# A two-layer conformer trunk: three opening products by rows, and attention corners without a padded key tile

## The chip, the core and the metric

The kernel runs on one core of one Trainium2 chip. A core has TensorE (PE, matrix products into PSUM), VectorE (DVE), ScalarE (ACT), GpSimd (POOL) and SyncE (SP, which here only issues DMA transfers). Each engine works through its own queue in order and waits for others by semaphores. The metric is the device time of one execution in microseconds. Three runs of the kernel before took 2230.79, 2237.22 and 2239.99 us; the median is 2237.22.

## The reference

The input is 512 frames of 1024 numbers; 16 learned meta tokens stand in front, so the stream `h` has 528 tokens. There are two layers, all in fp32:

```
h += 1/2 * (silu(n(h) @ w_gate) * (n(h) @ w_up)) @ w_down        # first feed-forward, width 2816
u = n(h);  q, k, v, a, b, g_sb, g_conv = split(u @ w_in)
A = stick_breaking_attention(q, k, v) @ w_attn_out               # 8 heads of 64
B = conv_module(a, b) @ w_conv_out                               # causal, 31 taps
h += (sigmoid(g_sb) * A + sigmoid(g_conv) * B) @ w_out
h += 1/2 * (silu(n(h) @ w_gate2) * (n(h) @ w_up2)) @ w_down2     # second feed-forward
out = n(h)[16:]                                                  # n is an RMS norm with gains
```

Stick-breaking attention: the weight of key s for query t is sigmoid(z_ts) times the product of (1 - sigmoid(z_tj)) over all j between s and t, strictly causal. So each block of scores goes through a softplus, and sums of it over later keys are taken off before the exponential.

## The kernel before

The stream lies with channels on partitions: `h[k]`, eight tiles of 128 channels by 528 tokens. Every fp32 product is three products of split operands: a number is cast to a shorter type (`wh`, `uh`: high part, ScalarE) and the rest is kept (`wl`, `ul`: low part, VectorE); hi x hi, hi x lo and lo x hi are added in PSUM. `split` (line 69) does this for a weight of 128 x 1024, `prepare` (line 279) for a tile of the stream with its gain; `prepare` also takes the square (`squares`, line 293), and the squares are added up in `nsum`, by GpSimd but for the last two of eight. A product with ones and a short chain on VectorE and ScalarE makes `rstd` of the sum. The norm's factor is applied to the products' results, so products start before it is known.

The feed-forward (`ffn`, line 413) goes over 22 blocks of 128 columns of `w_gate` and `w_up`. The first two (`PLAIN`) are plain: 48 products for a matrix and a block, 24 weight tiles by two token halves. The other blocks go in pairs through `quad` (line 470): seven groups of 24 products in place of eight, which need sums of weight tiles and sums of token halves (`sums`, line 329: per pair of stream tiles two activations, four short VectorE products and two splits). After blocks 4, 10, 16 and 22 follow the down products (`down`, line 526). In the first feed-forward all eight `prepare` stand first, then the four `sums` ahead of the plain blocks, which the scheduler puts in between.

The attention (`attend`, line 689) works on a pair of heads. Keys and queries are split into high and low parts, scores go in four pieces of 128 keys. The last 16 keys and the first 16 tokens are a corner of their own: GpSimd copies 64 x 16 pieces of `kf` into a zeroed tile `kz`, one plain fp32 product per column group gives the scores of both heads (lines 711 to 719), and a bf16 product of `identb` and `masksb` adds the mask. There are four head pairs in each of two layers, so eight corners.

A scheduler orders the instructions of each engine by priority and readiness; `priority(EARLY)` and `priority(LATE)` move a piece. Weights are fetched by SP into three buffers `wr` in the order of the list `units`, three units ahead of use. In PSUM, `ps` has two buffers and `pb` and `pe` have one each.

Of the kernel before, what the change touches and what calls it, by code (L numbers as in the profile page):

```python
# [7 lines left out]
F32 = mybir.dt.float32  # L8
# [16 lines left out]
PLAIN = 2  # L25
ORDER = (0, 4, 1, 5, 2, 6, 3, 7)
CONV = 512
# [3 lines left out]
EARLY = 3000  # L31
CONV_STEP = 4
# [21 lines left out]
def kernel(ctx, tc, hT, par, const, wg1, wu1, wd1, win, wao, wco, wout, wg2, wu2, wd2, out):  # L54
# [68 lines left out]
    for l in range(DEPTH):  # L123
        for fi, (wg, wu, wd) in enumerate(((wg1, wu1, wd1), (wg2, wu2, wd2))):
# [12 lines left out]
            for m in range(PLAIN):  # L137
                units += [((f"g{fi}", l, m), wg[l, m], 8), ((f"u{fi}", l, m), wu[l, m], 8)]
            m = PLAIN
# [7 lines left out]
    state = {"prep": 0, "use": 0, "fetch": 0, "out": 0, "sums": 0, "raw": 1}  # L147
# [3 lines left out]
    def pieces(n, block=None):  # L151

        key, src, nk = units[n]
        if nk in QUAD:
            wg, wu, m = src
            k, c = RAW_OF[block or nk]
            return [(4 * e, 4 * e + 4, w[m + c, :, 4 * k:4 * k + 4]) for e, w in enumerate((wg, wu))]
        return [(a, b, src[:, a:b]) for a, b in (((0, 2), (2, nk)) if n == 0 else ((0, nk),))]
# [9 lines left out]
    def fetch():  # L168
        while state["fetch"] < len(fetches) and state["out"] < state["raw"]:
# [25 lines left out]
    def prep_unit():  # L195
# [7 lines left out]
        if nk not in QUAD:  # L203
            raw = raws.pop(key)
            for a, b in ((0, 2), (2, nk)) if n == 0 else ((0, nk),):
                split(raw[:, a:b], hi[:, a:b], lo[:, a:b])
# [12 lines left out]
        if state["raw"] > 1:  # L219
            fetch()  # L220
# [20 lines left out]

    prm = cst.tile([P, N_PAR], F32, name="prm")
    nc.sync.dma_start(prm, par)
    h = [hpool.tile([P, T], F32, name=f"h{k}") for k in range(KD)]
    for n, k in enumerate(ORDER):
        nc.sync.dma_start(h[k], hT[:, k])
        if n in (0, 3):
            prep_unit()
    state["raw"] = RAW
# [10 lines left out]
    dve.tensor_copy(trir, cc[:, C_TRI:C_TRI + P])  # L260
    identb = cst.tile([P, P], BF16, name="identb")
    dve.tensor_copy(identb, ident)
    maskb = cst.tile([P, 240], BF16, name="maskb")
    dve.tensor_copy(maskb, cc[:, C_MASK:C_MASK + 240])
    masksb = cst.tile([64, 32], BF16, name="masksb")
    dve.tensor_copy(masksb, cc[:64, C_MS:C_MS + 32])
# [12 lines left out]
    def prepare(tp, k, ncol, st, mode=FULL, alloc=None):  # L279
# [10 lines left out]
        if alloc is not None and 0 <= k - 4 < 3:  # L290
            sums(alloc, k - 4, st, mode)

    def squares(tp, k, st, mode):
# [6 lines left out]
        else:  # L300
# [3 lines left out]
            eng = dve if n >= KD - 2 else pool  # L304
            eng.tensor_tensor(out=tri(st["sum"], mode), in0=tri(a, mode), in1=tri(sq, mode), op=ALU.add)
# [23 lines left out]
    def sums(alloc, kk, st, mode):  # L329
# [12 lines left out]
        parts = []  # L342
        for r in (r1, r2):
            hi, lo = (two(stile(kk, n), mode) for n in ("sh", "sl"))
            split(r, hi, lo)
            parts.append((hi, lo))
        st.setdefault("S", {})[kk] = parts
# [65 lines left out]
    def ffn(l, fi, st, mode, after):  # L413
# [3 lines left out]
        with tc.tile_pool(name=f"ffn{l}{fi}", bufs=1, reuse_waits="tile") as fp, \  # L417
# [8 lines left out]
            if first:  # L426
                for k in ORDER:
                    prepare(fp, k, 0, st)
# [27 lines left out]
            def gate_up(m):  # L456
                pg = plain("pe" if m else "ps", "g", m)[:, :, :TH]
                if m == 0:
                    norm["r"] = rms_rstd(fp, st, ptile("pb"), mode)
                pu = plain("pb" if m else "ps", "u", m)[:, :, :TH]  # L460
# [5 lines left out]
                parts(u, m)  # L466

# [94 lines left out]
            with tc.tile_pool(name=f"quad{l}{fi}", bufs=1, reuse_waits="tile") as sp:  # L562
                quads.update(pool=sp, of=(fi, l))
                fetch_sums()
                for m in range(PLAIN):
                    if m == 0:
                        for kk in range(0 if first else 3, 4):
                            sums(gtile, kk, st, mode)
                    gate_up(m)
                m = PLAIN  # L570
# [13 lines left out]
    def mixer(l, st, omode, after):  # L584
        last = omode == XO
        with ExitStack() as es:
# [53 lines left out]
            with tc.tile_pool(name=f"psm{l}", bufs=3, space=bass.MemoryType.PSUM, reuse_waits="tile") as psp, \  # L640
# [29 lines left out]
                with tc.tile_pool(name=f"att{l}", bufs=1, reuse_waits="tile") as ap_:  # L670
# [18 lines left out]
                    def attend(i, qf, kf, vf):  # L689
# [21 lines left out]
                        kz = ap_.tile([P, 2, P], F32, tag="kz", bufs=1, name="kz")  # L711
                        pool.memset(kz, 0.0)
                        zs = ztile()[:, 0, :]
                        for c, t0 in ((0, SEQ), (1, 0))[:ncor]:
                            for hh in range(2):
                                r = slice(64 * hh, 64 * hh + 64)
                                pool.tensor_copy(kz[r, c, 32 * hh:32 * hh + 16], kf[r, t0:t0 + 16])  # L717
                            pe.matmul(zs[:, c * 16:c * 16 + 16], kz[:, c, :], qf[:, t0:t0 + 16],
                                      start=(c == 0), stop=False, skip_group_check=True)
# [231 lines left out]
```

## Time and profile before

| | |
|---|---|
| median of three runs | 2237.22 us |
| the profiled execution | 2235.04 us |
| its span, first to last instruction | 2233.3 us |
| PE, DVE, ACT, POOL busy | 2190.7, 1618.3, 1037.6, 467.7 us |
| TensorE's mean granted clock | 0.994 |

All rows below are from the profiled execution, with times from the start of its span. A matmul's duration overlaps its neighbour's; the distance of starts tells the rate. A granted clock of 1 is 2.4 GHz, 0.5 is 1.2 GHz.

### The profile page before, as it was taken

The page shows a single profiled execution, that of the slowest core. Times are in us where ns is not written, and L with a number is a line of the kernel's source. Part 1 is how long each engine was busy: PE and PEld are TensorE (multiplying, and loading weights), DVE is VectorE, ACT ScalarE, POOL GpSimd, SP SyncE. Part 2 cuts the span into 40 slices and gives each one's busy share as a digit, 9 for nine tenths or more (in the row PEclk, how much of TensorE's full clock was granted, in tenths as well). Part 3 has the DMA queues.
Part 4 walks back from the last instruction along what each step waited for, and adds up shares of the span by engine and source line. Part 5 has one row for each costly group of instructions (what it writes and reads, how often), then busy time and mean ns, then how long its engine had stood idle before and what let it go on. Part 6 is the DMA issues. An engine that isn't in the chain of part 4 may idle for free.

```text
span 2233.3 us, 39375 instructions
## 1 busy us (share of the span) xinstructions
PE 2190.7 (98%) x16140; PEld 2065.1 (92%) x16140; DVE 1618.3 (72%) x2113; ACT 1037.6 (46%) x1448; POOL 467.7 (21%) x394
## 2 busy tenths in 40 slices
PE   7999999999999999999999999999999999999997
PEld 6999999988899999999999999999777788999896
DVE  8767686877777768576887676868777777776684
ACT  6344345355535444353554443552665365444353
POOL 3322321100000132313123223211000002322222
PEclk9999999999999999999999999999999999999999
DMA  7565533211122275474265654332111225575532
GB/s 220 151 164 136 145 102 116 86 38 48 55 75 89 92 180 150 131 181 128 86 162 150 170 144 131 107 112 86 48 48 57 89 92 145 150 179 140 151 107 74
DMA packets 120261, 263.26 MB, mean 118 GB/s; under 512 B 13200, under 2 KB 15504, under 8 KB 120080
## 3 DMA queue, kind: packets, MB, share of 16 engines
q1 hardware_dynamic: 96240, 217.99, 29.9%
q0 software_dynamic: 23040, 41.95, 11.7%
q8 instruction: 127, 2.08, 0.4%
q10 hardware_dynamic: 800, 0.79, 0.1%
q14 instruction: 54, 0.44, 0.1%
HBM read 258.58 MB, written 2.10 MB: 117 GB/s over the span
## 4 chain that ended last, share of the span: by engine, by line
PE 93%; DVE 3%; POOL 1%; issue 1%; ACT 1%; DMA 0%; DVEq 0%; SPq 0%; POOLq 0%; ACTq 0%
PE ps L604 24%; PE ps L484 15%; PE pb L484 15%; PE ps L238 10%; PE pb L238 6%; PE pe L238 6%; PE pe L484 5%; PE z L604 2%; PE po L787 2%; PE ps L449 2%; PE z L777 1%; PE pe L449 1%; PE pb L449 1%; POOL kz L717 1%; PE z L760 1%
## 5 line engine op out<-in xcount | busy, mean ns | idle before, releaser
L71 ACT CAST wh<-wr 128x1024 fp32r<-128x1024 f32 (+3 forms) x369 | 352.1, 954 | 600.4 <-PE ps L604 178.5
L72 DVE TENSOR_TENSOR wl<-wr,wh 128x1024 fp32r<-128x1024 f32 (+3 forms) x369 | 439.4, 1191 | 73.0 <-ACT wh L71 67.3
L71 ACT CAST wh<-s 128x1024 fp32r<-128x1024 f32 x160 | 167.9, 1050 | 280.0 <-DVE s L214 84.6
L72 DVE TENSOR_TENSOR wl<-s,wh 128x1024 fp32r<-128x1024 f32 x160 | 218.5, 1365 | 58.8 <-ACT wh L71 58.0
L544 POOL TENSOR_TENSOR h<-h,dt 128x528 f32<-128x528 f32 (+1 forms) x96 | 179.6, 1875 | 252.3 <-DVE dt L542 252.3
L604 PE MATMUL ps<-uh,wh 128*128 128x264 f32 (+1 forms) x864 | 223.0, 315 | 0.4 <-DVE kf L677 0.3
L604 PE MATMUL ps<-ul,wh 128*128 128x264 f32 (+1 forms) x864 | 218.8, 310 | 0.0
L604 PE MATMUL ps<-uh,wl 128*128 128x264 f32 (+1 forms) x864 | 215.4, 309 | 0.0
L192 POOL DMA_DIRECT2D s<-wg x80 | 74.6, 933 | 542.6 <-DMA s<-wg 265.9
L632 DVE SCALAR_TENSOR_TENSOR y<-uc,prm,y 128x528 f32<-128x528 f32 (+1 forms) x240 | 183.4, 764 | 4.7
L484 PE MATMUL pb<-sh,wh 128*128 128x264 f32 (+1 forms) x640 | 181.8, 284 | 2.7 <-ACT pb L503 2.7
L484 PE MATMUL ps<-uh,wh 128*128 128x264 f32 (+1 forms) x640 | 181.3, 283 | 1.0 <-DVE g L463 1.0
L484 PE MATMUL pb<-sh,wl 128*128 128x264 f32 (+1 forms) x640 | 182.2, 285 | 0.0
L484 PE MATMUL pb<-sl,wh 128*128 128x264 f32 (+1 forms) x640 | 182.0, 284 | 0.0
L484 PE MATMUL ps<-uh,wl 128*128 128x264 f32 (+1 forms) x640 | 181.3, 283 | 0.0
L484 PE MATMUL ps<-ul,wh 128*128 128x264 f32 (+1 forms) x640 | 181.3, 283 | 0.0
L604 PEld LDWEIGHTS ps<-uh,wh 128*128 128x128 f32 x864 | 145.3, 191 | 20.9 <-issue 10.5
L604 PEld LDWEIGHTS ps<-ul,wh 128*128 128x128 f32 x864 | 145.5, 192 | 13.0 <-issue 6.8
L604 PEld LDWEIGHTS ps<-uh,wl 128*128 128x128 f32 x864 | 143.6, 191 | 12.1 <-issue 5.9
L238 PE MATMUL ps<-al,wh 128*128 128x264 f32 (+1 forms) x616 | 142.7, 301 | 0.5 <-DVE al L72 0.2
L238 PE MATMUL ps<-ah,wh 128*128 128x264 f32 (+1 forms) x616 | 141.8, 300 | 0.0
L238 PE MATMUL ps<-ah,wl 128*128 128x264 f32 (+1 forms) x616 | 141.7, 300 | 0.0
(276 smaller groups left out, 6042.9 us busy)
## 6 DMA issues: line engine op xcount, KB each, us to landing
wr<-wd SPq DMA_DIRECT2D x96, 384.0 KB, 3.6
wr<-win SPq DMA_DIRECT2D x72, 512.0 KB, 3.3
wr<-wg SPq DMA_DIRECT2D x120, 256.0 KB, 3.0
wr<-wu SPq DMA_DIRECT2D x120, 256.0 KB, 3.5
s<-wg SPq DMA_DIRECT2D x80, 256.0 KB, 4.5
s<-wu SPq DMA_DIRECT2D x80, 256.0 KB, 5.3
s<-wg POOLq DMA_DIRECT2D x80, 256.0 KB, 5.2
s<-wu POOLq DMA_DIRECT2D x80, 256.0 KB, 6.8
```

The costliest lines, as they stand in the source:

```text
L71: act.copy(hi, x)
L72: dve.tensor_tensor(out=lo, in0=x, in1=f(hi), op=ALU.subtract)
L192: pool.dma_start(t[:, a:b], src, accum_op=ALU.add)
L238: pe.matmul(ps[:, c, :n], wt[:, k0 + k, :], xt[:, s:s + n], start=(k == 0 and pi == 0), stop=(k == nk - 1 and pi == 2))
L449: pe.matmul(ps[:, e, :TH], wt[:, k, :], xt[:, s], start=(k == ORDER[0] and pi == 0), stop=(k == ORDER[-1] and pi == 2))
L484: pe.matmul(ps[:, e, :TH], wt[:, 4 * e + kk, :], xt, start=start and kk == 0 and pi == 0, stop=kk == 3 and pi == 2, skip_group_check=True)
L544: pool.tensor_tensor(out=tri(h[j], mode), in0=tri(h[j], mode), in1=tri(t, mode), op=ALU.add)
L604: pe.matmul(ps, wt[:, k0 + k, :], xt[:, s], start=(n == 0 and pi == 0), stop=(n == nk - 1 and pi == 2))
L632: t = dve.scalar_tensor_tensor(out=y, in0=uc[i][:, c0 + k:k + T], scalar=col(w0 + k), in1=y, op0=ALU.mult, op1=ALU.add)
L717: pool.tensor_copy(kz[r, c, 32 * hh:32 * hh + 16], kf[r, t0:t0 + 16])
L760: pe.matmul(z[:, hh, :n], KH[hh][:, ks], qq, start=True, stop=False, skip_group_check=True)
L787: pe.matmul(po[c, q0 - META:q0 - META + n], v[:, t, c], a[:, hh, :], start=False, stop=(t == 0), skip_group_check=True)
```

## The change

In the first feed-forward the first three matrices (gate and up of block 0, gate of block 1) are computed together, row tile by row tile, as the stream arrives. Stream tiles and weight pieces are fetched in five steps (`BEGIN`), in that order. Four blocks are plain there, and the `sums` come with blocks 2 and 3. All square sums go to VectorE, in every feed-forward and mixer. In the other feed-forwards `head` takes the place of `gate_up`, with `pb` and `pe` exchanged, and the sums of the next block have a later priority (`SOON`). The corner products read `kf` and `qf` directly, one product for a head and column group, and the mask product opens the buffer.

```diff
-PLAIN = 2
+PLAIN, PLAIN_FIRST = 2, 4
+BEGIN = ((0, 1), (1, 2), (2, 4), (4, 6), (6, 8))
+SOON = 150
...
     prm = cst.tile([P, N_PAR], F32, name="prm")
-    nc.sync.dma_start(prm, par)
+    nc.scalar.dma_start(prm[:, :N_NORM], par[:, :N_NORM])
     h = [hpool.tile([P, T], F32, name=f"h{k}") for k in range(KD)]
-    for n, k in enumerate(ORDER):
-        nc.sync.dma_start(h[k], hT[:, k])
-        if n in (0, 3):
-            prep_unit()
-    state["raw"] = RAW
+    begin = [wpool.tile([P, 8, P], F32, tag="wr", bufs=RAW, name="wr") for _ in range(3)]
+    for a, b in BEGIN:
+        for k in range(a, b):
+            nc.sync.dma_start(h[k], hT[:, k])
+        for raw, (_, src, _) in zip(begin, units):
+            nc.sync.dma_start(raw[:, a:b], src[:, a:b])
+    state.update(prep=3, use=3, fetch=3)
+    nc.sync.dma_start(prm[:, N_NORM:], par[:, N_NORM:])
...
         if alloc is not None and 0 <= k - 4 < 3:
-            sums(alloc, k - 4, st, mode)
+            with priority(SOON):
+                sums(alloc, k - 4, st, mode)
...
-            eng = dve if n >= KD - 2 else pool
-            eng.tensor_tensor(out=tri(st["sum"], mode), in0=tri(a, mode), in1=tri(sq, mode), op=ALU.add)
+            dve.tensor_tensor(out=tri(st["sum"], mode), in0=tri(a, mode), in1=tri(sq, mode), op=ALU.add)
...
-            def gate_up(m):
-                pg = plain("pe" if m else "ps", "g", m)[:, :, :TH]
-                if m == 0:
-                    norm["r"] = rms_rstd(fp, st, ptile("pb"), mode)
-                pu = plain("pb" if m else "ps", "u", m)[:, :, :TH]
+            def evac(m, pg, pu):
                 g = gtile()
...
+            def head():
+
+                pg = plain("ps", "g", 0)
+                norm["r"] = rms_rstd(fp, st, ptile("pe"), mode)
+                sums(gtile, 3, st, mode)
+                evac(0, pg[:, :, :TH], plain("ps", "u", 0)[:, :, :TH])
+                pg = plain("pb", "g", 1)
+                evac(1, pg[:, :, :TH], plain("pe", "u", 1)[:, :, :TH])
+
+            def first_head():
+
+                ws = [tuple(wpool.tile([P, 8, P], F32R, tag=n, bufs=4, name=n) for n in ("wh", "wl")) for _ in begin]
+                pss = [ptile(t) for t in ("ps", "ps", "pb")]
+                for a, b in BEGIN:
+                    for k in range(a, b):
+                        prepare(fp, k, 0, st)
+                    for raw, (hi, lo) in zip(begin, ws):
+                        split(raw[:, a:b], hi[:, a:b], lo[:, a:b])
+                    for k in range(a, b):
+                        xh, xl = st["u"][k]
+                        for ps, (hi, lo) in zip(pss, ws):
+                            for pi, (wt, xt) in enumerate(((hi, xh), (hi, xl), (lo, xh))):
+                                for e, s in enumerate(toks):
+                                    pe.matmul(ps[:, e, :TH], wt[:, k, :], xt[:, s], start=(k == 0 and pi == 0),
+                                              stop=(k == KD - 1 and pi == 2))
+                norm["r"] = rms_rstd(fp, st, ptile("pe"), mode)
+                g = fp.tile([P, T], F32, tag="up", bufs=3, name="up")
+                act.copy(th(g), pss[2][:, :, :TH])
+                evac(0, pss[0][:, :, :TH], pss[1][:, :, :TH])
+                evac(1, th(g), plain("pb", "u", 1)[:, :, :TH])
+                for m, tags in ((2, ("ps", "ps")), (3, ("pe", "ps"))):
+                    pg, pu = (plain(t, n, m)[:, :, :TH] for t, n in zip(tags, "gu"))
+                    evac(m, pg, pu)
+                    for kk in range(2 * m - 4, 2 * m - 2):
+                        sums(gtile, kk, st, mode)
...
-                        kz = ap_.tile([P, 2, P], F32, tag="kz", bufs=1, name="kz")
-                        pool.memset(kz, 0.0)
                         zs = ztile()[:, 0, :]
+                        pe.matmul(zs[:, :w], identb[:64, :], masksb[:, :w], start=True, stop=False, skip_group_check=True)
                         for c, t0 in ((0, SEQ), (1, 0))[:ncor]:
                             for hh in range(2):
                                 r = slice(64 * hh, 64 * hh + 64)
-                                pool.tensor_copy(kz[r, c, 32 * hh:32 * hh + 16], kf[r, t0:t0 + 16])
-                            pe.matmul(zs[:, c * 16:c * 16 + 16], kz[:, c, :], qf[:, t0:t0 + 16],
-                                      start=(c == 0), stop=False, skip_group_check=True)
-                        pe.matmul(zs[:64, :w], identb[:64, :64], masksb[:, :w], start=False, stop=False,
-                                  skip_group_check=True)
+                                pe.matmul(zs[32 * hh:32 * hh + 16, c * 16:c * 16 + 16], kf[r, t0:t0 + 16],
+                                          qf[r, t0:t0 + 16], start=False, stop=False, skip_group_check=True)
```

TensorE's queue at the very start, before and then now; `ps_270` is the gate of block 0 before, and now `ps_156`, `ps_157` and `pb_158` are the three matrices (`x2`: both token halves).

```order
L449 MATMUL ps_270<-uh0_133,wh_87 128x264 x2
L449 MATMUL ps_270<-ul0_134,wh_87 128x264 x2
L449 MATMUL ps_270<-uh0_133,wl_88 128x264 x2
L449 MATMUL ps_270<-uh4_139,wh_87 128x264 x2
L449 MATMUL ps_270<-ul4_140,wh_87 128x264 x2
L449 MATMUL ps_270<-uh4_139,wl_88 128x264 x2
```

```order
L489 MATMUL ps_156<-uh0_159,wh_150 128x264 x2
L489 MATMUL ps_156<-ul0_160,wh_150 128x264 x2
L489 MATMUL ps_156<-uh0_159,wl_151 128x264 x2
L489 MATMUL ps_157<-uh0_159,wh_152 128x264 x2
L489 MATMUL ps_157<-ul0_160,wh_152 128x264 x2
L489 MATMUL ps_157<-uh0_159,wl_153 128x264 x2
L489 MATMUL pb_158<-uh0_159,wh_154 128x264 x2
L489 MATMUL pb_158<-ul0_160,wh_154 128x264 x2
L489 MATMUL pb_158<-uh0_159,wl_155 128x264 x2
L489 MATMUL ps_156<-uh1_189,wh_150 128x264 x2
```

One tile of the stream now serves 18 products before the next is needed; before it served 6.

VectorE's queue after the three matrices, now: `wl_422` is the low part of `u` of block 1, `wl_428` and `wl_434` those of block 2, `wl_440` that of the gate of block 3; `nt` and `rstd` are the norm, `g_404` the first evacuation, which frees `ps_156`.

```order
L74 TENSOR_TENSOR wl_422<-wr_415,wh_421 128x1024
L74 TENSOR_TENSOR wl_428<-wr_417,wh_427 128x1024
L365 TENSOR_SCALAR nt_393<-pe_389 128x528
L74 TENSOR_TENSOR wl_434<-wr_419,wh_433 128x1024
L366 TENSOR_TENSOR nt_394<-rstd_390 128x528
L367 SCALAR_TENSOR_TENSOR nt_394<-nt_394,nt_393 128x528
L368 SCALAR_TENSOR_TENSOR rstd_390<-nt_394,rstd_390 128x528
L74 TENSOR_TENSOR wl_440<-wr_425,wh_439 128x1024
L461 TENSOR_TENSOR g_404<-ps_156,rstd_390 128x528
```

Before, the products of the token halves stood among the steps of the norm; now three weight splits do:

```order
L341 SCALAR_TENSOR_TENSOR g_238<-h6_81,prm_73,g_237 128x264
L361 TENSOR_TENSOR nt_345<-rstd_341 128x528
L72 TENSOR_TENSOR sl_246<-g_237,sh_245 128x528
L362 SCALAR_TENSOR_TENSOR nt_345<-nt_345,nt_344 128x528
L72 TENSOR_TENSOR sl_250<-g_238,sh_249 128x528
L341 SCALAR_TENSOR_TENSOR g_254<-h3_78,prm_73,g_253 128x264
```

The `g` and `sl` rows here belong to the sums of token halves, which now come with blocks 2 and 3.

TensorE's queue at the first corner of the first layer, before and then now; `z_5208` and `z_5229` are the corner's buffers, `ps_5132`, `ps_5133`, `ps_5155` and `ps_5156` the projection of `v` around it.

```order
L604 MATMUL ps_5133<-ul0_4140,wh_4931 128x264
L604 MATMUL ps_5133<-uh0_4139,wl_4932 128x264
L604 MATMUL ps_5133<-uh4_4146,wh_4931 128x264
L718 MATMUL z_5208<-qf_4998,kz_5206 128x16 x2
L720 LDWEIGHTS identb_116
L720 MATMUL z_5208<-masksb_120,identb_116 64x32
L604 MATMUL ps_5133<-ul4_4147,wh_4931 128x264
L604 MATMUL ps_5133<-uh4_4146,wl_4932 128x264
```

```order
L634 MATMUL ps_5156<-uh0_4162,wh_4954 128x264
L634 MATMUL ps_5156<-ul0_4163,wh_4954 128x264
L634 MATMUL ps_5156<-uh0_4162,wl_4955 128x264
L746 MATMUL z_5229<-qf_5021,kf_5084 16x16 x4
L634 MATMUL ps_5156<-uh4_4169,wh_4954 128x264
L634 MATMUL ps_5156<-ul4_4170,wh_4954 128x264
L634 MATMUL ps_5156<-uh4_4169,wl_4955 128x264
L634 MATMUL ps_5155<-uh1_4221,wh_4954 128x264
```

The place is the same to one product; the operands are `kf` and `qf` instead of `kz` and `qf`, and the mask product has moved ahead, out of this piece.

## Rows read from the trace of the kernel before

**Rows 1.** The page: busy time of the engines, and TensorE's strip.

```profile
PE 2190.7 (98%) x16140; PEld 2065.1 (92%) x16140; DVE 1618.3 (72%) x2113; ACT 1037.6 (46%) x1448; POOL 467.7 (21%) x394
...
PE   7999999999999999999999999999999999999997
```

**Rows 2.** Stretches: length, busy (count) of five engines, granted clock, DMA share, GB/s.

```profile
0.00:5.39 5.39, 0.00 (x0) 0.00 (x0) 0.94 (x3) 2.47 (x4) 0.55 (x9) 1.00 0.65 179
5.39:65.81 60.42, 51.53 (x366) 48.93 (x367) 51.25 (x74) 36.76 (x59) 19.38 (x17) 0.97 0.77 217
```

**Rows 3.** TensorE's waits over the span: total us, times, longest.

```profile
PE z L718 <- POOL kz L717: 11.9, 8, 2.1
```

**Rows 4.** The chain of waits in the opening: start, us, what.

```profile
49.37 4.64 PE pb L484 x24
...
65.81 6.05 PE ps L238 x48
71.86 2.93 PE pb L238 x24
```

**Rows 5.** Timeline at the first corner: start, us, engine, line, operation, idle before.

```profile
439.37 0.76 DVE L677 SCALAR_TENSOR_TENSOR kf<-ps,rstd 128x264 f32<-128x264 f32 x2
...
439.94 2.68 POOL L717 COPY kz<-kf 64x16 f32<-64x16 f32 x4 [9.77 <-DVE kf L677]
...
442.68 0.62 PE L718 MATMUL z<-qf,kz 128*128 128x16 f32 x4 [2.07 <-POOL kz L717]
...
443.39 0.59 PE L604 MATMUL ps<-ul,wh 128*128 128x264 f32 x1
```

**Rows 6.** Stretches after the first and the last of four corner waits.

```profile
443.39:446.74 3.35, 3.35 (x16) 3.35 (x16) 1.46 (x3) 0.83 (x3) 0.32 (x1) 0.52 0.18 71
...
1556.00:1559.60 3.60, 3.60 (x19) 3.54 (x19) 3.12 (x6) 1.19 (x4) 0.32 (x1) 0.54 0.46 150
```

**Rows 7.** Timeline of the opening.

```profile
4.10 0.73 ACT L284 ACTIVATE uh<-h,prm 128x528 fp32r<-128x528 f32 x1 [2.07 <-DMA h<-hT]
...
4.87 0.77 DVE L285 SCALAR_TENSOR_TENSOR ul<-h,prm,uh 128x528 fp32r<-128x528 f32 x1 [1.59 <-ACT uh L284]
4.93 0.41 ACT L71 CAST wh<-wr 128x256 fp32r<-128x256 f32 x1
5.25 0.64 ACT L296 ACTIVATE sq<-h 128x528 f32<-128x528 f32 x1
...
5.55 0.42 DVE L72 TENSOR_TENSOR wl<-wr,wh 128x256 fp32r<-128x256 f32 x1
...
19.92 0.69 DVE L305 TENSOR_TENSOR nsum<-nsum,sq 128x528 f32<-128x528 f32 x1
```

**Rows 8.** Groups of the opening by shape: count, busy us, mean ns.

```profile
L71 ACT CAST wh<-wr 128x1024 fp32r<-128x1024 f32 x6 | 6.1, 1041 | 0.0
...
L72 DVE TENSOR_TENSOR wl<-s,wh 128x1024 fp32r<-128x1024 f32 x4 | 4.9, 1221 | 0.1
```

**Rows 9.** DMA issues: count, size, median us from issue to landing.

```profile
wr<-wg SPq DMA_DIRECT2D x7, 512.0 KB, 3.2
```

**Rows 10.** Timeline at the boundary of the layers, GpSimd and VectorE.

```profile
1111.82 1.60 POOL L305 TENSOR_TENSOR nsum<-sq 128x528 f32<-128x528 f32 x1 [7.38 <-ACT sq L296]
...
1112.18 1.94 DVE L341 SCALAR_TENSOR_TENSOR g<-h,prm,g 128x264 f32<-128x264 f32 x2
...
1131.71 0.89 DVE L341 SCALAR_TENSOR_TENSOR g<-h,prm,g 128x264 f32<-128x264 f32 x2
```

**Rows 11.** Timeline in the third head pair: the buffer of its corner.

```profile
518.44 0.34 PE L780 MATMUL z<-sl,trir 128*128 128x400 f32 x1
...
518.83 0.93 ACT L95 ACTIVATE a<-z,bias 128x800 f32<-128x800 f32 x1 [4.62 <-PE z L780]
...
526.14 1.04 ACT L71 CAST sh<-sp 128x1024 fp32r<-128x1024 f32 x1
...
531.31 0.39 PE L779 MATMUL z<-sh,trir 128*128 128x512 f32 x1
```

More of the change, by code (lines that the diff above doesn't have):

```diff
@@ L136 @@
                 units += [(("wo", l, j), wout[l, j], 8) for j in ORDER]
-            for m in range(PLAIN):
+            m = PLAIN if l or fi else PLAIN_FIRST
+            for m in range(m):
                 units += [((f"g{fi}", l, m), wg[l, m], 8), ((f"u{fi}", l, m), wu[l, m], 8)]
-            m = PLAIN
+            m += 1
             for gi, (m0, m1) in enumerate(GROUPS):
@@ L146 @@
     RAW = 3
-    state = {"prep": 0, "use": 0, "fetch": 0, "out": 0, "sums": 0, "raw": 1}
+    state = {"prep": 0, "use": 0, "fetch": 0, "out": 0, "sums": 0}
     ready, raws = {}, {}
@@ L157, in pieces @@
             return [(4 * e, 4 * e + 4, w[m + c, :, 4 * k:4 * k + 4]) for e, w in enumerate((wg, wu))]
-        return [(a, b, src[:, a:b]) for a, b in (((0, 2), (2, nk)) if n == 0 else ((0, nk),))]
+        return [(0, nk, src[:, :nk])]
     fetches = []
@@ L168, in fetch @@
     def fetch():
-        while state["fetch"] < len(fetches) and state["out"] < state["raw"]:
+        while state["fetch"] < len(fetches) and state["out"] < RAW:
             n = fetches[state["fetch"]]
@@ L204, in prep_unit @@
             raw = raws.pop(key)
-            for a, b in ((0, 2), (2, nk)) if n == 0 else ((0, nk),):
-                split(raw[:, a:b], hi[:, a:b], lo[:, a:b])
+            split(raw[:, :nk], hi[:, :nk], lo[:, :nk])
             state["out"] -= 1
@@ L218, in prep_unit @@
                 state["out"] -= d in RAW_OF
[L219 to L220 removed]
+        fetch()
     def unit(*key):
@@ L259 @@
     trir = cst.tile([P, P], F32R, name="trir")
-    dve.tensor_copy(trir, cc[:, C_TRI:C_TRI + P])
     identb = cst.tile([P, P], BF16, name="identb")
-    dve.tensor_copy(identb, ident)
     maskb = cst.tile([P, 240], BF16, name="maskb")
-    dve.tensor_copy(maskb, cc[:, C_MASK:C_MASK + 240])
     masksb = cst.tile([64, 32], BF16, name="masksb")
-    dve.tensor_copy(masksb, cc[:64, C_MS:C_MS + 32])
+    with priority(LATE):
+        dve.tensor_copy(trir, cc[:, C_TRI:C_TRI + P])
+        dve.tensor_copy(identb, ident)
+        dve.tensor_copy(maskb, cc[:, C_MASK:C_MASK + 240])
+        dve.tensor_copy(masksb, cc[:64, C_MS:C_MS + 32])
     l4 = cc[:64, C_L4:C_L4 + 2 * P]
@@ L341, in sums @@
             dve.scalar_tensor_tensor(out=o, in0=x, scalar=g, in1=y, op0=ALU.mult, op1=op)
-        parts = []
+        S = st.setdefault("S", {})[kk] = []
         for r in (r1, r2):
@@ L345, in sums @@
             split(r, hi, lo)
-            parts.append((hi, lo))
-        st.setdefault("S", {})[kk] = parts
+            S.append((hi, lo))
     def rstd_from(tp, src, ps, n, eps, epscol, mode, dst):
@@ L564, in ffn @@
                 fetch_sums()
[L565 to L570, printed above, removed]
+                (first_head if first else head)()
+                m = PLAIN_FIRST if first else PLAIN
                 for gi, (m0, m1) in enumerate(GROUPS):
```

3 lines of the change are left out of this document (removed).

## The prediction

> **What bounds the kernel now.** I read the shares of the engines first. TensorE is busy for 98% of the span, VectorE, the next, for 72% [rows 1]. So time can only leave where TensorE stands still, where it runs at the lower clock, or where a product goes away. The strip of 40 slices shows it below nine tenths only in the first slice and the last [rows 1], but a wait of 2 us does not show in a slice of 56. So I read TensorE's wait list next. Its first entry is the corner products of the attention, which wait for GpSimd's copies into the padded key tile: 11.9 us in eight waits [rows 3]. Last I read the chain of waits through the opening [rows 4].
>
> **The opening.** The same point in both kernels is the start of the first down product. It is at 65.81 us [rows 4]; TensorE starts at 5.39 us, and in the 60.42 us between runs 366 products and is busy for 51.53 us [rows 2]. At full speed 24 products take 2.93 us, 0.122 each [rows 4], so 366 need 44.7 us: 15.7 us are lost to waits and to the lower clock. The last such loss is 4.64 us for 24 products after a wait [rows 4].
>
> What the change adds to this: blocks 2 and 3 are computed plainly, 4 x 48 products where the quad has 7 x 24, so 24 more, 2.9 us. What it takes away: the four sums of token halves, with 16 short VectorE products and 8 splits, no longer stand ahead of the first quad. They move behind block 2 and block 3, and the two extra blocks cover them.
>
> The new first phase has 144 products (three matrices, eight row tiles of the stream). ScalarE needs for two tiles of the stream with their three weight pieces 2 x (0.73 + 0.64) and 3 x 0.41 = 4.0 us; VectorE needs 2 x 0.77, 2 x 0.69 for the square sums that now are its own, and 3 x 0.42: 4.2 us [rows 7]. TensorE needs 36 x 0.122 = 4.4 us. The three are matched, and TensorE is slightly the last. The first activation starts at 4.10 us [rows 7], as the first tile lands; with it, the square and a first small cast (0.3 us, estimated by a line through the casts of 256 columns [rows 7] and of 1024 [rows 8]) TensorE starts at 5.8. The first 18 products run at the lower level, as after a wait (16 products in 3.35 us, 0.21 each [rows 6]): 3.8 us, to 9.6. The other 126 take 15.4 us: 25.0, and 25.3 with a short wait for the last low parts.
>
> Then the queue is exposed once more. The next weights (`u` of block 1) go into a buffer that is free only when VectorE has split the last piece of the first matrix, at about 21.0. They land 3.2 us later [rows 9] and are cast in 1.04 [rows 8]: 25.3. ScalarE then copies `pb` out (0.63, as the square) and casts the next weights: 27.1. From there VectorE does, in its order, a weight split, one step of the norm, a split, three steps of the norm, a split and the first evacuation: 3 x 1.22 [rows 8] and 5 x 0.70 [rows 7] = 7.2, to 34.3. TensorE starts `u` of block 1 at 26.1, ends it at 32.0, does ten products of `g` of block 3 that the new order puts in between (waiting about 1 us for their low weights), and begins `g` of block 2 when `ps` is free, at 34.3. By then 144 + 48 + 10 = 202 of the 384 are done; the other 182 take 22.2 us. That gives 56.5, and 57.0 with hand-overs. The down product wants the parts of block 3 only after 30 products, 3.7 us, and VectorE has some 2.5 us of work for them, so no wait is added there. The opening gains 65.8 - 57.0 = **8.8 us**. Bounds: with no wait and full clock 5.4 + 388 x 0.122 = 52.7, a gain of 13.1; with the first phase wholly at the lower level (144 x 0.21 = 30 us instead of 19.5), a loss of 10.7 against my figure, so a loss of 1.9 against before.
>
> **The corners.** Before, VectorE brings out `kf` at 439.37 to 440.13, GpSimd copies four pieces from 439.94 to 442.62, and TensorE's product starts at 442.68 [rows 5]. Without the padded tile only `kf` is waited for. In the new order nine products (1.1 us) stand between the end of the `k` projection and the corner in the first head pair; `kf` needs 0.9. So I take all 11.9 us [rows 3] as gone. After four of the eight waits the clock falls: in the first and the last of these four stretches the granted clock is 0.52 and 0.54, the level of 1.2 GHz; 16 products take 3.35 us and 19 take 3.60, where 0.122 each would make 1.95 and 2.32 [rows 6]. That is 1.3 us each, 5.2 in all, and goes with the waits.
>
> Against it: from the first corner product to the next projection there are now 0.71 us [rows 5], with four passes of a product and the mask. The new form has eight passes (four in the second layer), each of half the rows. If each costs what one does now (0.14 us), the corner is 0.5 us longer in the first layer and 0.25 in the second, 3 us over eight; if half, nothing. I take 1.2. The mask product now stands ahead of the corner and opens the buffer, so it waits for the exponential that reads that buffer. That one ends 1.32 us after the last product into it started (518.44, then 518.83 + 0.93 [rows 11]); in the new order 0.2 + 9 x 0.12 = 1.3 us lie between. Behind the mask product TensorE's projection is queued, so a miss costs TensorE directly: 0.3 us in all. What is late next is the split of the last piece of the pair before: its cast ends at 527.18 for a product at 531.31 [rows 11]. TensorE comes there up to 2.1 [rows 3] + 1.3 us sooner, at 527.9: 0.7 us are left, so I take no new wait. The corners give 17.1 - 1.5 = **15.6 us**; bounds 17.1, and 6 if at each of the six later pairs the split is late by 1.6 us.
>
> **The square sums.** Outside the opening 25 additions move from GpSimd to VectorE. TensorE is full there, which hides them; uncovered they would cost 25 x 0.69 = 17 us. But an addition on GpSimd is not free for VectorE: beside one (1111.82, 1.60 us) two short products take 1.94 us, where the same two take 0.89 alone [rows 10]. VectorE gives up 1.05 us there and now would pay 0.69. I take 0, between -1 and +4.
>
> **Sum.** 8.8 + 15.6 = 24.4 us off 2235.04, the profiled execution (span 2233.3): 2210.6. The median of the three runs is 2.2 us higher, so I forecast 2213 us.
>
> **Two rules of the Trainium skill, weighed.** One 512 KB transfer lands in 3.2 us [rows 9], and the opening before moves 179 GB/s up to 5.39 us [rows 2]. The Trainium skill ("DMA: Bandwidth & Descriptors", section Bandwidth) says that transfers of 64 KB or less are ruled by their descriptors, and gives 0.95 us for one of 64 KB. By that page the six small weight pieces would take an estimated 5.7 us one after another. No run here shows pieces of that size; if the page rules, the second rival below decides. The granted clock of 0.52 after a wait [rows 6] agrees with "TensorE: Matmul & The Clock Gate", section HAM oscillation, in the Trainium skill, that idle gaps put the array back to the lower level; the last rival below rests on the row.
>
> **The rivals.**
> - The new opening is fed too late: transfers in small pieces and three matrices at once delay each of the five steps, and 57 becomes 66. For it: 23 transfers are issued before anything else, and the first tile alone took until 4.10 [rows 7]. Against it: the last step's tiles, with 3.7 MB in all, are wanted at 16.5 us (19.65 less 2 x 1.37 and 0.41), 226 GB/s from the start, where before 179 GB/s came up to 5.39 and 217 after it at a share of 0.77, so up to 282 [rows 2]. Time: 2237.2 - 15.6 = 2222.
> - TensorE's waits at the corners move on to the softplus chain, where only 0.7 us are spare. Gain at the corners 5 instead of 15.6: 2237.2 - 13.8 = 2223.
> - The corners wait as before, because `kf` and not the copies is the last to come, and the change does not do what it says. Against it: `kf` is out 2.5 us before the product starts [rows 5]. Time: 2237.2 - 8.8 = 2228.
> - Slower: the first phase has a short wait at each of its five steps, and TensorE stays at 1.2 GHz through all 384 products. Each costs 0.21 - 0.122 = 0.088 us more, beyond the 18 that I counted; from 277 products on the whole gain is gone, and with 366 it is 2213 + 32 = 2245. Against it: before, 366 products took 60.42 us with all waits, where they would need 77 at 0.21, and the granted clock over them was 0.97 [rows 2].
>
> **How the numbers follow.** My forecast 0.66 (2203 to 2220), late opening 0.17, softplus 0.10, corners unchanged 0.03, lower clock 0.04. Half a per cent, about what a measurement can tell from no change, is 11 us: 2226. The first three are faster by more, but for some of the tails of the second and third: faster 0.87, same 0.09, slower 0.04. The range reaches from 2203 (both best bounds give 2237.2 - 30.2 = 2207, and the runs of before lie up to 6 us from their median) over the second and third case to 2226.
>
> **What would show it.** Right: the first down product starts near 57 us; the wait for `kz` has no successor above 0.5 us; the granted clock of the attention stretches is 1.00. Wrong: long idle times of TensorE before 25 us ended by transfers or casts; products on `sh` and `trir` that wait for ScalarE; low clock after 12 us.

## The result, and the profile after

The changed kernel takes 2211.43 us (median of four runs, 2210.14 to 2212.06) where the kernel before, beside it on the same chip, took 2234.96 (four runs, 2230.79 to 2239.99): a ratio of 0.9893, 95% interval 0.987 to 0.9916. The forecast was 2213. Its two large terms were both wrong, in opposite directions: the opening gave less than it said, the corners more.

The page of the profile after (span 2210.2 us, granted clock 0.996; before 2233.3 and 0.994), for [rows 1]:

```profile
PE 2183.2 (99%) x16188; PEld 2061.1 (93%) x16188; DVE 1618.1 (73%) x2148; ACT 1035.5 (47%) x1453; POOL 391.8 (18%) x323
```

TensorE's busy time (which counts slow products at their full length) fell by 7.5 us and the span by 23.1, so most of what left was standing still. GpSimd lost 76 us, VectorE's sum is the same to 0.2 us.

Stretches of the opening, for [rows 2] (length, busy of PE, PEld, DVE, ACT, POOL, granted clock, DMA share, GB/s):

```profile
5.24:25.40 20.16, 20.14 (x148) 19.63 (x148) 14.16 (x34) 12.14 (x28) 3.69 (x4) 1.00 0.92 284
25.40:63.46 38.06, 33.35 (x242) 32.71 (x243) 24.70 (x37) 20.28 (x31) 3.46 (x4) 0.91 0.62 163
```

The first phase, 5.24 to 25.40 with four products of the norm at its end, is full: no wait. Its start is slow all the same (TensorE's timeline: start, us, what):

```profile
5.24 0.81 PE L489 MATMUL ps<-uh,wh 128*128 128x264 f32 x2 [5.24 <-ACT wh L73]
...
8.86 0.41 PE L489 MATMUL ps<-uh,wh 128*128 128x264 f32 x2
...
24.34 1.05 PE L357 MATMUL pe<-nsum,ones 128*128 128x264 f32 x4
```

The first 18 products take 3.6 us, the other 126 take 15.5, 0.123 each. The forecast had 3.8 and 15.4, so this part of its sum holds; the phase ends at 24.3 instead of 25.0 because it starts 0.6 earlier. The column of the granted clock reads 1.00 here and does not show the slow start; the distance of the starts does: 0.22 a product up to 8.05, as in the slow stretches below. The loss is in the second stretch: 38.06 us with 33.35 busy and a clock of 0.91.

TensorE's waits over the span, for [rows 3]:

```profile
PE ps L489 <- ACT wh L73: 5.2, 1, 5.2
PE pt L760 <- DVE vf L707: 2.1, 4, 0.6
PE pb L451 <- ACT up L493: 2.1, 1, 2.1
PE pe L451 <- ACT wh L73: 2.1, 1, 2.1
```

The corner wait of 11.9 us is gone and has no successor at the corners: `pt` with its 2.1 us stood in the list before too. The waits on `pb` and `pe` (L451) lie in the opening. Between its first product and the first down product TensorE waits 4.7 us now, where it waited 8.6 before, at other places.

The chain of waits through the opening, for [rows 4] (start, us, what):

```profile
19.14 6.75 DMA wr<-wu
...
25.91 1.05 ACT wh L73
...
26.99 1.24 DVE wl L74
...
28.24 8.08 DMA wr<-wg
...
38.76 1.55 PE pe L451 x6
...
63.46 5.82 PE ps L239 x48
```

The first down product starts at 63.46 where it was 65.81 before and 57.0 in the forecast. Two weight transfers stand in the chain, of 6.75 and 8.08 us; the forecast had 3.2. Behind the first stand its cast (L73) and its split (L74), which frees the buffer for the second transfer; behind the second a cast, a split and the product that waits for them. So the two delays add up.

What lay in the DMA queues from 12 to 45 us (share of 16 engines; then count, size, median us from issue to landing), for [rows 9]:

```profile
q1 hardware_dynamic: 3321, 6.95, 61.6%
q0 software_dynamic: 979, 1.80, 31.2%
...
wr<-wu SPq DMA_DIRECT2D x3, 512.0 KB, 8.2
...
wr<-wg SPq DMA_DIRECT2D x2, 512.0 KB, 7.8
```

The q0 row is transfers that add: GpSimd adds the second block's weights into the tiles `s1` and `s3` for the first two quads, whose first blocks SyncE fetches just before. At a share of 61.6 and 31.2% the queues are nearly full, and 512 KB take about 8 us.

Two of the opening's waits are followed by low clock, for [rows 6]:

```profile
28.00:33.00 5.00, 4.99 (x29) 4.78 (x28) 3.55 (x5) 3.56 (x5) 0.29 (x1) 0.66 1.08 301
39.00:43.00 4.00, 4.00 (x22) 4.00 (x22) 3.91 (x6) 2.58 (x5) 1.17 (x2) 0.58 0.62 160
```

In 5.00 us at a clock of 0.66 and in 4.00 at 0.58, 1.7 us are lost each time ((1 - 0.66) x 5.00).

The first corner, for [rows 5]:

```profile
436.67 0.77 DVE L707 SCALAR_TENSOR_TENSOR kf<-ps,rstd 128x264 f32<-128x264 f32 x2
...
437.71 0.27 PE L746 MATMUL z<-qf,kf 64*16 64x16 f32 x8
...
437.91 0.39 PE L634 MATMUL ps<-uh,wh 128*128 128x264 f32 x1
```

From the first of eight passes to the next projection it is 0.20 us; before it was 0.71, after a wait. The two stretches of attention that hold the eight corners run at a granted clock of 1.00:

```profile
430.00:640.00 210.00, 208.72 (x1498) 181.11 (x1497) 164.64 (x249) 118.98 (x177) 3.57 (x4) 1.00 0.16 56
1530.00:1720.00 190.00, 188.51 (x1064) 147.15 (x1063) 149.99 (x210) 113.65 (x162) 4.02 (x4) 1.00 0.16 59
```

### The profile page after: what moved, and what is told of

Its sections match the earlier page's. It is cut to its first block, busy times and chain, and to the rows that moved or that the text cites. A ratio compares the mean times of both kernels' runs of the same rounds, so it can differ in the third digit from the quotient of the medians.

```text
span 2210.2 us, 39393 instructions
## 1 busy us (share of the span) xinstructions
PE 2183.2 (99%) x16188; PEld 2061.1 (93%) x16188; DVE 1618.1 (73%) x2148; ACT 1035.5 (47%) x1453; POOL 391.8 (18%) x323
## 4 chain that ended last, share of the span: by engine, by line
PE 95%; DVE 2%; DMA 1%; ACT 1%; issue 1%; POOL 0%; SPq 0%; DVEq 0%; ACTq 0%; POOLq 0%
PE ps L634 25%; PE ps L518 15%; PE pb L518 15%; PE ps L239 10%; PE pb L239 6%; PE pe L239 6%; PE pe L518 5%; PE ps L451 2%; PE z L634 2%; PE po L813 2%; PE z L803 1%; PE pe L451 1%; PE pb L451 1%; DVE wl L74 1%; PE z L786 1%
## 5 line engine op out<-in xcount | busy, mean ns | idle before, releaser
L73 ACT CAST wh<-wr 128x1024 fp32r<-128x1024 f32 (+4 forms) x381 | 354.4, 932 | 605.3 <-PE ps L634 168.3
L74 DVE TENSOR_TENSOR wl<-wr,wh 128x1024 fp32r<-128x1024 f32 (+4 forms) x381 | 441.2, 1160 | 82.6 <-ACT wh L73 77.2
L73 ACT CAST wh<-s 128x1024 fp32r<-128x1024 f32 x156 | 163.7, 1049 | 275.3 <-DVE s L216 87.7
L74 DVE TENSOR_TENSOR wl<-s,wh 128x1024 fp32r<-128x1024 f32 x156 | 212.5, 1362 | 59.3 <-ACT wh L73 58.6
L634 PE MATMUL ps<-uh,wh 128*128 128x264 f32 (+1 forms) x864 | 220.5, 312 | 0.3 <-DVE kf L707 0.3
L634 PE MATMUL ps<-uh,wl 128*128 128x264 f32 (+1 forms) x864 | 214.4, 308 | 0.0
L634 PE MATMUL ps<-ul,wh 128*128 128x264 f32 (+1 forms) x864 | 214.0, 307 | 0.0
L518 PE MATMUL ps<-ul,wh 128*128 128x264 f32 (+1 forms) x624 | 177.3, 284 | 0.0
L518 PE MATMUL pb<-sl,wh 128*128 128x264 f32 (+1 forms) x624 | 176.9, 283 | 0.0
L518 PE MATMUL ps<-uh,wl 128*128 128x264 f32 (+1 forms) x624 | 176.8, 283 | 0.0
L518 PE MATMUL pb<-sh,wl 128*128 128x264 f32 (+1 forms) x624 | 176.8, 283 | 0.0
L518 PE MATMUL pb<-sh,wh 128*128 128x264 f32 (+1 forms) x624 | 176.4, 283 | 0.0
L518 PE MATMUL ps<-uh,wh 128*128 128x264 f32 (+1 forms) x624 | 176.1, 282 | 0.0
L634 PEld LDWEIGHTS ps<-uh,wl 128*128 128x128 f32 x864 | 141.6, 188 | 13.4 <-issue 7.2
```

The source lines that it names most:

```text
L73: act.copy(hi, x)
L74: dve.tensor_tensor(out=lo, in0=x, in1=f(hi), op=ALU.subtract)
L518: pe.matmul(ps[:, e, :TH], wt[:, 4 * e + kk, :], xt, start=start and kk == 0 and pi == 0, stop=kk == 3 and pi == 2, skip_group_check=True)
L634: pe.matmul(ps, wt[:, k0 + k, :], xt[:, s], start=(n == 0 and pi == 0), stop=(n == nk - 1 and pi == 2))
```

## The experiments

**The opening.** Theory: the sums' transfers crowd the weights. Rivals: the three fetch buffers set the landing; the small pieces do.

*Sums late.* The fetch of the first two pairs of sum tiles stands behind the plain weights.

```diff
-                fetch_sums()
+                if not first:
+                    fetch_sums()
...
                     for kk in range(2 * m - 4, 2 * m - 2):
                         sums(gtile, kk, st, mode)
+                fetch_sums()
...
-                nc.sync.dma_start(t[:, a:b], src)
+                d = nc.sync.dma_start(t[:, a:b], src)
+                if at[:2] == [0, 0]:
+                    tc.add_manual_dep(d.ins, newest[0].ins.name, NOSYNC, reason="behind the plain weights")
```

(`newest` is the last weight fetch issued; the dependency orders SyncE's queue only.)

> The first feed-forward's first two pairs of sum tiles (s1, s3: eight fetches by SyncE and eight accumulating ones by GpSimd, 256 KB each) are issued behind the fetches of the plain weights instead of at 13.23 to 41.84 us. Theory A (these transfers crowd the plain blocks' weights, which land 6.75 to 8.08 us after their issue): the weights land within 4 us, the three waits of 2.1 us on casts and the low-clock stretches behind them go, the first down product starts at 57 to 58.5 us instead of 63.46, and the time falls by 5 to 6 us to about 2206. Theory B (three fetch buffers: no fetch can be issued before a buffer is split at 19.14 us, and the chain fetch, cast, product is what is late): the landings stay above 6 us, the first down product stays at 62 to 64 us and the time at 2210 to 2213.

Measured: 2204.73 us (2204.5 to 2206.05), ratio 0.9863, 0.9848 to 0.9879. The queues from 12 to 45 us, and the chain:

```profile
wr<-wu SPq DMA_DIRECT2D x3, 512.0 KB, 4.5
wr<-wg SPq DMA_DIRECT2D x2, 512.0 KB, 3.7
```

```profile
26.62 5.93 PE pb L454 x48
...
56.32 5.82 PE ps L242 x48
```

The weights land in 4.5 and 3.7 us, the chain holds nothing but TensorE's own work, and the down product starts at 56.32. Theory A holds, B falls: the buffers are the same three. This version beats both kernels: its runs lie below every run of after.

*Without the adding transfers* of the first two quads:

```diff
-            for a, b, src in pieces(n, "w12"):
+            for a, b, src in pieces(n, "w12") if at[:2] != [0, 0] or at[2] >= 8 else ():
```

> Leaves out the eight accumulating transfers of the first two quads (their products use the first block's weights alone); the eight fetches by SyncE stay where they are. Theory A1 (the accumulating transfers are what crowds): first down product at 57 to 59 us, the time about 2205 to 2207. Theory A2 (it is the bytes, 2 MB of plain fetches as much as 2 MB of accumulating ones): about half of it, first down product at 60 to 62 us, the time about 2208 to 2210. Theory B (fetch buffers): 62 to 64 us, 2210 to 2213.

Measured: 2205.06 us (2204.14 to 2208.47), first down product at 57.01. The queues, and the chain:

```profile
wr<-wu SPq DMA_DIRECT2D x3, 512.0 KB, 3.3
```

```profile
57.01 5.82 PE ps L239 x48
```

*The same transfers, writing instead of adding:*

```diff
-                pool.dma_start(t[:, a:b], src, accum_op=ALU.add)
+                pool.dma_start(t[:, a:b], src, **({} if at[:2] == [0, 0] and at[2] < 8 else dict(accum_op=ALU.add)))
```

> The eight GpSimd transfers of the first two quads stay, with the same bytes in the same places, but write instead of adding (their products use the second block's weights alone). Theory A1 (adding in the transfer is what costs: their time a byte in the trace is twice that of the other queue): first down product at 58 to 60 us. Theory A2 (bytes in the same queues): 62 to 63.5 us, as after. Theory B: 62 to 64 us.

Measured: 2206.91 us (2206.34 to 2209.45), first down product at 58.44. The queues, and the chain:

```profile
q0 software_dynamic: 640, 2.10, 20.3%
...
wr<-wu SPq DMA_DIRECT2D x3, 512.0 KB, 5.2
```

```profile
58.44 5.82 PE ps L239 x48
```

So in steps: the plain fetches of the sums cost the opening 0.7 us (57.01 - 56.32), the same bytes again by GpSimd's queue 1.4 more, and that they add 3.0 to 5.0 more (to 61.44 and 63.46 in the two profiles of after). A1 is right: of the crowding most comes with the adding. But 1.7 and 3.4 us of this last step are low clock behind the waits, of which the other three openings have none; the delay itself is 1.3 to 1.6 us, about that of the bytes.

Two limits. The steps come from one profile each, and the slow first products alone (12 of them in after, 24 with the sums late) move an opening by up to 1.2 us; the times, 2204.73, 2205.06, 2206.91 and 2210.33 to 2211.43, are in the same order. And by the packet both kinds cost the same, 0.17 us of one engine (31.2% of 16 engines for 33 us over 979 packets, 20.3% over 640), but the adding ones hold 1.8 KB each and the writing ones 3.3. Whether the adding or the smaller packets cost is not tested.

*Coarse opening,* four steps in place of five:

```diff
-BEGIN = ((0, 1), (1, 2), (2, 4), (4, 6), (6, 8))
+BEGIN = ((0, 2), (2, 4), (4, 6), (6, 8))
```

> The opening in four steps of two rows each instead of five (1, 1, 2, 2, 2). Theory (weights behind the first phase are late, not the pieces of the first phase): first product later by 0.5 to 1.5 us, the end of the first phase (25.4 us) as much later or less, the first down product at 63 to 64.5 us, the time within 2 us of 2211. Rival (the small 64 KB pieces keep the queues busy, and with it what stands behind them): u's weights of block 1 are issued before 18.5 us, the first down product at 60 to 62 us, the time 2208 to 2209.5.

Measured: 2210.22 us (2208.56 to 2211.52). The chain:

```profile
19.26 9.47 DMA wr<-wu
...
59.94 5.82 PE ps L239 x48
```

The weight transfer in the chain takes even longer than those of after (9.47 us; the median of the three is 6.2, in after 8.2), so the small pieces are not what crowds. The down product, at 59.94, is earlier than either expectation: here no low-clock stretch followed the wait, which is worth 1.7. The next run takes the crowding away.

*Coarse opening with late sums* (both edits).

> The version with the late sum transfers, and the opening in four steps of two rows instead of five. By the run of the coarse opening alone (2210.2 against 2211.4, first product of block 0 later by 1.4 us): with nothing crowded behind the first phase the later start costs 1 to 1.5 us: 2205.5 to 2206.5. Rival (fewer transfers are done sooner, and the start is no later in the end): 2203.5 to 2205.

Measured: 2206.14 us (2205.88 to 2207.12); first down product at 57.04, 0.72 later than with five steps, and the time 1.4 us longer, on another chip. So five steps are a little better here.

*The changed kernel again.*

> The changed kernel once more, beside the other two on the same chip, and with a second profile of its opening: 2210 to 2212. The opening of three versions that share it started the first down products at 61.4 to 62.4 us where after's own profile had 63.3: if the difference is one low-clock stretch of 1.7 us more or less, this profile has one or two such stretches and 61.4 to 63.5.

Measured: 2210.33 us (2210.08 to 2211.37); first down product at 61.44 with one low-clock stretch, where the first profile had two and 63.46. Here the first weights landed in 3.58 us, and only the second transfer was late:

```profile
24.93 9.46 DMA wr<-wg
...
61.44 4.61 PE ps L239 x38
```

**The corners.** *The corner part alone,* put into the kernel before (the last piece of the diff of the change).

> The kernel before with the corner part alone. By the trace of after (evacuations of the second head pair's k earlier by 2.7 at the first corner and by 20.1 at the eighth, of which the opening has 2.35) the corner part is worth 17 to 21 us: 2214 to 2218 against 2235. By the forecast's term it is 15.6 us: 2219. If what is gained at the corners is partly the square sums' move: 10 to 14 us, 2221 to 2225.

Measured: 2214.05 us (2213.77 to 2216.3) against 2234.07, ratio 0.9904, 0.9891 to 0.9918. The corners are worth 20.0 us, not 15.6. The granted clock of these runs says how much of it is low clock: its mean is 0.9945 in the 15 runs of before and 0.9972 in the four of this version, 12.2 and 6.1 us lost ((1 - clock) times the span), so about 6.1 of the 20.0.

*The padded tile back* in the changed kernel (that piece undone).

> The kernel after with the padded key tile back, opening and square sums as in after. By the trace of after the rest is worth 2 to 4 us: 2231 to 2233 against 2235. By the forecast's terms (opening 8.8): 2226.

Measured: 2233.72 us (2230.45 to 2237.66) against 2234.07: 0.9995, 0.9983 to 1.0006, within neither expectation. Two of its waits, and two of its stretches of low clock:

```profile
PE z L748 <- POOL kz L747: 11.9, 8, 2.1
...
PE pe L451 <- ACT wh L73: 4.1, 1, 4.1
```

```profile
438.76:443.76 5.00, 5.00 (x29) 4.96 (x28) 1.47 (x3) 0.83 (x3) 0.32 (x1) 0.66 0.10 40
449.76:453.76 4.00, 4.00 (x20) 3.72 (x20) 1.98 (x5) 0.66 (x3) 0.31 (x1) 0.57 0.40 135
```

The wait on `kz` is back to the tenth. The first down product is at 61.82, 4.0 us earlier than before, and that gain is then lost: its attention loses 12.0 us to low clock in seven stretches of 1.7, before's 6.8 in four, of which these are the first and the last:

```profile
442.37:447.37 5.00, 4.69 (x26) 4.63 (x27) 2.43 (x5) 1.17 (x4) 0.57 (x2) 0.66 0.27 101
...
1555.07:1560.07 5.00, 4.33 (x23) 4.27 (x24) 4.05 (x7) 2.07 (x6) 0.93 (x2) 0.66 0.33 108
```

Three stretches more, 5.1 us. The clock of all runs agrees: the mean is 0.9926 in the 11 runs of this version, 16.4 us lost, 4.2 more than before. So the gain of the opening is still there, and low clock takes it back. The stretch at 449.76 comes after two short waits, for `vf`, and not after a corner's:

```profile
447.15 0.44 PE L764 MATMUL pt<-cc,vf 128*128 128x128 f32 x2 [0.64 <-DVE vf L707]
448.09 0.44 PE L764 MATMUL pt<-cc,vf 128*128 128x128 f32 x2 [0.50 <-DVE vf L707]
```

*Small products, but from GpSimd's tile,* so that the wait is kept:

```diff
+                        kz = ap_.tile([P, 2, P], F32, tag="kz", bufs=1, name="kz")
+                        pool.memset(kz, 0.0)
...
+                                pool.tensor_copy(kz[r, c, 32 * hh:32 * hh + 16], kf[r, t0:t0 + 16])
...
-                                pe.matmul(zs[32 * hh:32 * hh + 16, c * 16:c * 16 + 16], kf[r, t0:t0 + 16],
+                                pe.matmul(zs[32 * hh:32 * hh + 16, c * 16:c * 16 + 16], kz[r, c, 32 * hh:32 * hh + 16],
```

> The kernel after, with its small corner products, but reading the keys from the tile that GpSimd copies (filled and copied as before), so that the wait is kept and only the form of the products differs from the padded version. If the whole gain is the wait and the clock behind it: the waits of 1.4 to 1.6 us at each corner are back, and the time is that of the version with the padded tile, 2229 to 2233. If the form of the products has a share of 3 to 5 us (8 passes of 64 x 16 took 0.27 us in all, the padded ones 0.7 us from the first corner product to the next projection): 2226 to 2229. If the wait costs nothing by itself: 2211 to 2214.

Measured: 2225.56 us (2222.67 to 2226.88), 15.2 more than after again and 14.1 more than after. Its first corner, and its wait:

```profile
435.36 2.68 POOL L748 COPY kz<-kf 64x16 f32<-64x16 f32 x4 [9.79 <-DVE kf L707]
...
437.39 0.21 PE L752 MATMUL z<-qf,kz 64*16 64x16 f32 x2 [1.38 <-POOL kz L748]
...
438.10 0.26 PE L752 MATMUL z<-qf,kz 64*16 64x16 f32 x6 [0.49 <-POOL kz L748]
...
438.29 0.39 PE L634 MATMUL ps<-ul,wh 128*128 128x264 f32 x1
```

```profile
PE z L752 <- POOL kz L748: 6.8, 12, 1.4
```

The first two passes start while GpSimd still copies the rest, so the wait is in two pieces, 1.4 us at the longest. In the attention of this profile no stretch of low clock follows. So a wait costs much by itself. The time lies just under the expectation's second case, which puts the rest, 8.2 us to the padded version, on the form of the products. The granted clock says otherwise: 0.9962 in the mean of these five runs against 0.9926, or 8.0 of the 8.2 us. The next run measures the form by itself.

*The padded form without the wait:* VectorE fills the tile, right behind `kf`, ahead of the splits.

```diff
+                                dve.tensor_copy(kz[r, c, 32 * hh:32 * hh + 16], kf[r, t0:t0 + 16])
                         QS, KH, KL = [], [], []
...
+                            pe.matmul(zs[:, c * 16:c * 16 + 16], kz[:, c, :], qf[:, t0:t0 + 16],
+                                      start=(c == 0), stop=False, skip_group_check=True)
```

> The kernel after with the padded key tile and the padded products back, but VectorE fills the tile right behind the evacuation of k instead of GpSimd, so that the waits of 2.1 us and the low-clock stretches behind them should be gone and only the form of the products is that of before. If the form is worth what lies between the version with GpSimd's padded tile (2233.7) and the one with GpSimd's tile and small products (2225.6): 2218 to 2220. If those 8 us are the longer wait and the low-clock stretches that only it brings (each costs 1.7 us in the windows), and the form itself costs 0.4 to 0.5 us a corner (0.71 us against 0.20 from its first product to the next projection): 2213 to 2216, with waits on kz of under 0.5 us. By the forecast's term (the padded form cheaper by 1.2 us in all): 2210 to 2211, and more by the wait that is left.

Measured: 2213.89 us (2213.66 to 2214.77), 3.6 more than after again. Its first corner, its wait, and its one stretch of low clock in the attention:

```profile
434.88 0.71 DVE L726 COPY kz<-kf 64x16 f32<-64x16 f32 x4
...
435.74 0.59 PE L749 MATMUL z<-qf,kz 128*128 128x16 f32 x4 [0.18 <-DVE kz L726]
...
436.38 0.39 PE L634 MATMUL ps<-uh,wl 128*128 128x264 f32 x1
```

```profile
PE z L749 <- DVE kz L726: 0.6, 2, 0.4
```

```profile
445.00:449.00 4.00, 3.96 (x17) 3.69 (x18) 1.83 (x5) 0.66 (x3) 0.30 (x1) 0.57 0.37 135
```

Four copies take VectorE 0.71 us, where GpSimd takes 2.68. Of the 3.9 us between the profiled spans (2212.1 and 2208.2), 1.7 are the low-clock stretch and 0.6 the wait. That leaves 1.6 us for the form of the products, 0.2 a corner, with the mask product behind them again and with whatever VectorE's extra copies delay, which is not tested apart: the second expectation holds. The forecast had the small form dearer by 1.2.

**The square sums** back on GpSimd, outside the opening:

```diff
-            dve.tensor_tensor(out=tri(st["sum"], mode), in0=tri(a, mode), in1=tri(sq, mode), op=ALU.add)
+            state["nsq"] = state.get("nsq", 0) + 1
+            eng = dve if n >= KD - 2 or state["nsq"] < KD else pool
+            eng.tensor_tensor(out=tri(st["sum"], mode), in0=tri(a, mode), in1=tri(sq, mode), op=ALU.add)
```

> The kernel after with the square sums of all but the opening back on GpSimd (six of eight of each of the later norms). By the forecast the move is worth nothing: 2210 to 2213, between the feed-forwards 1.60 us pieces on GpSimd beside VectorE's 1.94. Rival (GpSimd, freed of them, answers sooner at the boundaries): 2213 to 2217. Rival (VectorE is relieved): 2207 to 2210.

Measured: 2212.39 us (2210.93 to 2214.76). The boundary of the layers in after, and in this version:

```profile
1095.00:1130.00 35.00, 35.00 (x286) 34.87 (x286) 34.13 (x55) 24.70 (x39) 1.80 (x3) 1.00 0.46 149
```

```profile
1095.00:1130.00 35.00, 34.88 (x281) 34.39 (x280) 34.22 (x48) 23.43 (x37) 9.59 (x6) 1.00 0.42 134
```

VectorE is busy for 34.13 us in the one and 34.22 in the other: what it no longer adds it loses beside GpSimd. TensorE is full in both. The move is worth nothing that these runs can tell.

## Why the prediction was right, and where it was wrong

**The total** came from two errors that cancel: forecast 8.8 + 15.6 = 24.4 us, measured 23.5 between medians and 23.1 between spans. That 2213 came so close to 2211.43 is luck.

**The opening, 8.8 forecast, 2.35 in the profile (4.4 in the second one).** The step that failed is "They land 3.2 us later [rows 9]". That row is a median over seven transfers, taken without asking what shared the queues with these. In the new opening `u` of block 1 and the gate of block 3 took 6.75 and 8.08 us (3.58 and 9.46 in the second profile), since GpSimd's adding transfers run at that time. Each late landing became a wait of TensorE, and low clock behind it: low clock after 12 us, one of the prediction's own signs of being wrong, came at 28 and at 39. With these transfers moved away the rest of that step-by-step sum holds: 56.32 against 57.0. The first rival foresaw an opening fed too late, and its 66 is nearer to the 63.46 than the forecast's 57. But it put that on the small pieces and from the start; the first phase had no wait, and the coarse opening lands its weights as late.

**The corners, 15.6 forecast, 20.0 measured.** That all of the 11.9 us go was right, and that nothing at the softplus takes their place. Two terms were mis-sized. The clock: four stretches at 1.7 us are 6.8 and not 5.2, since the rows chosen for the price covered only part of each stretch. The products: forecast to cost 1.2 us more, and 0.3 with the buffer; the run with VectorE's tile puts them at 1.6 less. 11.9 + 6.8 + 1.6 = 20.3, against 20.0. The 20.0 is measured by the corner part alone, and its low clock by the runs' clocks too (6.1); how the rest divides between wait and form is argued, since in the version with small products from GpSimd's tile the waits do not simply add up (see below).

**The square sums, 0 forecast:** right, for the reason given.

**The rivals:** none decided as it stood. The slower one, 1.2 GHz through the 384 opening products, is refuted by the 126 products in 15.5 us; of it only the two slow stretches came. The rule on small transfers that the prediction weighs from the Trainium skill ("DMA: Bandwidth & Descriptors", section Bandwidth) belongs to the first rival and not, as written, to the second. The page has it for transfers under 64 KB, and the six smallest weight pieces are 64 KB. They landed in 2.7 us (median), and after its first product TensorE waited for none of them, so the rule did not decide.

**Open:** why the version with the padded tile has seven stretches of low clock in its attention where the kernel before, with the same waits, has four. The number also changes from run to run. The kernel before spreads over 12.3 us in 15 runs (2227.85 to 2240.14), after again over 1.3 in four, and the granted clocks on record show that this spread is low clock: 0.998 in the fastest of the 15, 0.992 in the slowest, a difference of 13.4 us (correlation of time and clock -0.97). What sets the number is not known. In the version with small products from GpSimd's tile, waits of 6.8 us cost 13.1 us of span (2221.3 against 2208.2). Over six stretches from one corner to the next TensorE is also busy 3.3 us longer there (231.04 against 227.69 us); the rest is not accounted for. Without its low clock, the padded version with its 11.9 us of waits is no more than about 1 us slower than this one.

## What to carry to other kernels

Before a landing time is put into a sum, look at what else is in the DMA queues just then, above all transfers that add; a prefetch that is wanted tens of us later belongs behind the fetches that are wanted next. A wait of TensorE of one to two us can cost as much again by the low clock behind it, so price a wait with the whole stretch that follows it, until the clock is back. A forecast that comes out right is no proof of its terms: only the landmark in the profile (63.46 for 57.0) and the run with one part alone showed that both were off. And compare the granted clocks of two versions before a difference between them is put on their instructions: here it was 8.0 of 8.2 us once.

## What the runs showed of the hardware

- Transfers that add took 5.7 us of all 16 engines for a MB (31.2% of 33 us for 1.80 MB), the same transfers writing 3.2 (20.3% for 2.10 MB); by the packet both took 0.17 us of one engine. Beside them 512 KB of weights took 8.2 us to land, beside the writing ones 5.2, with neither 3.3.
- Each stretch of low clock cost about the same, 1.7 us, after waits as different as 3.9 us in the opening (after again) and 0.64 and 0.50 in the attention (padded tile back). Behind the 1.4 us waits of the small products from GpSimd's tile there was none in the profile.
- The first products of an execution came 0.22 us apart, the pace of 1.2 GHz, 12 of them in after and 24 with the sums late, while the trace's granted clock read 1.00.
- Four 64 x 16 fp32 products, eight passes in the trace, each product in its own 16 rows and columns of one buffer, took 0.20 us from the first to the next projection.
